# A transformer block's MLP: the second product by Strassen's seven as well, and its weight blocks prepared once in DRAM

## The chip, the core and the metric

One core of a Trainium2 chip runs one fused kernel. The metric is the device time of one execution in microseconds (us). TensorE (PE) does the matmuls, its weight loads stand as PEld; VectorE is DVE, ScalarE is ACT, GpSimd is POOL, SyncE is SP. SP, ACT and POOL also issue the DMAs, each from its own instruction queue.

## What is computed

The reference is one layer of a diffusion block over 2048 latent tokens of 1024 channels, with 256 context tokens. Cut to the part that changes:

```python
x   = x + g1 * mixed                                  # mixed: Fourier branch + neighbourhood attention, gated, projected
hx2 = modulate(rms_norm(x, norm2_g), sh2, sc2)        # 2048 x 1024
a   = relu(hx2 @ w_mlp1)                              # w_mlp1: 1024 x 4096
x   = x + g2 * ((a * a) @ w_mlp2)                     # w_mlp2: 4096 x 1024
```

Everything ahead of it (modulation vectors, the input projection, the Fourier transform, the attention, the gated merge) is computed by the same kernel.

## The kernel before, in words

**The stages.** The kernel runs through an input stage (projections of all tokens, pair by pair in `run_pair`), the Fourier transforms, the attention, a merge stage and the MLP. `merge` takes tiles t = 0 to 7 of 256 tokens: `attn_out(t)` gates and merges the branches, `out_proj` multiplies by w_out and adds the residual, `norm_T(t)` normalises, transposes and writes the operands of the MLP to DRAM (`hcd`).

**Numbers in halves.** Every fp32 operand is split into an f16 high and an f16 low part, so one logical matmul is three (`mm3`, L78: high by high, high by low, low by high). `halve` (L1446 on ACT, L1447 on DVE) makes the two parts of a weight block, with a power-of-two scale from `msc`.

**Seven products.** The first MLP product uses Strassen's scheme in Winograd's form: both operands are cut into 2 by 2 blocks, seven block products are formed from sums and differences of blocks, and sums of the seven give the four output blocks. `norm_T` makes the seven token operands (`put`, `total`). `load_w1` makes the seven weight operands of one pair of 128 hidden columns: one 1 MB DMA, four sums (L1425) and seven splits. `mlp1` runs the seven products (`product`, twelve matmuls of 128x512 each), adds them (`plus`, L1457), and makes relu, square and the f16 parts (`squared`, L1471 to L1475).

**The second product** is plain. `load_w2` splits 128 rows of w_mlp2, `mlp2` multiplies. Tokens go in two halves of 1024; in each half the hidden columns go in groups of four blocks of 128: two units of `mlp1`, then sixteen PSUM tiles (`order2`) of twelve matmuls, each added to an accumulator in SBUF (`acc`). The weights are loaded, summed and split again for the second half of the tokens.

**What sets the order.** A scheduler orders each engine's instructions when the program is built; `tc.issue_after` pins some behind others, the MLP's matmuls among them. Each engine then executes its list in order. The side work of the input stage (`side_work`: modulation vectors, maxima of the MLP weights) is a generator; every `tick()` in `run_pair` advances it, at `pace` 3 (three steps per two ticks) for the second pair and 2 (one per tick) after it. `mmp` and `p2p` are PSUM pools of four tiles each, so a product can start when the fourth product ahead of it has been read out.

Of the kernel before, what the change touches and what calls it, by code (L numbers as in the profile page):

```python
# [32 lines left out]
WTOP = 32768.0  # L33
# [3 lines left out]
ATOP = 181.0  # L37

PRODUCTS = (0, 5, 6, 4, 3, 2, 1)
# [20 lines left out]
def dit_block(ctx: ExitStack, tc: tile.TileContext, a, out, taps=None, upto=9):  # L60
# [54 lines left out]
    hcd = scratch("hcd", [2, 7, 128, 4, 1024], F16)  # L115
# [166 lines left out]
    def side_work():  # L282
# [67 lines left out]
        for i, top in enumerate((BTOP, BTOP, WTOP, ATOP)):  # L350
            dve.tensor_scalar(out=m[:, i:i + 1], in0=m[:, i:i + 1], scalar1=1.0e-12, scalar2=2.0 / top, op0=ALU.max, op1=ALU.mult)
# [7 lines left out]
        dve.tensor_scalar(out=g2r, in0=g2r, scalar1=msc[:, 4:5], scalar2=None, op0=ALU.mult)  # L359

# [969 lines left out]
    def norm_T(t, q_=sp):  # L1330
# [19 lines left out]
        def put(c, src):  # L1350
# [3 lines left out]
            q_.dma_start(hcd[t // 4, c, :, t % 4], o.rearrange("p o k t -> p (o k t)"))  # L1354
# [36 lines left out]
    load_x1()  # L1391
    for t in range(NT - 2):
        out_proj(t, 0)
        out_proj(t, 1)
        for _ in attn_out(t + 2, mmp, pg):
            pass
        norm_T(t)
    pm.release()
# [8 lines left out]
    w1, w2 = a["w_mlp1"][0], a["w_mlp2"][0]  # L1407

    def load_hc(half, part):
        r = {}  # L1410
        for c in (PRODUCTS[:4], PRODUCTS[4:])[part]:
            r[c] = (pr if part else pl).tile([128, 4, 2, 4, 128], F16, tag=f"hc{c}", name=f"hc{half}_{c}")
            sp.dma_start(r[c].rearrange("p s o k t -> p s (o k t)"), hcd[half, c])
        return r

    def load_w1(half, f, p_):

        nm = f"{half}_{f}"
        wt = pl.tile([128, KT, 256], F32, tag="w1r", name=f"w1r{nm}", bufs=2)
        sp.dma_start(wt, w1[:, f * 128:(f + 2) * 128].rearrange("(k p) n -> p k n", p=128))  # L1420
        a11, a12, a21, a22 = (wt[:, 4 * k:4 * k + 4, i * 128:(i + 1) * 128] for i in range(2) for k in range(2))

        def total(c, x, y, op):
            r = pl.tile([128, 4, 128], F32, tag="ws", name=f"ws{nm}_{c}", bufs=3)
            dve.tensor_tensor(out=r, in0=x, in1=y, op=op)  # L1425
            return r

        r = {}

        def put(c, src):  # L1430
            r[c] = p_.tile([128, 2, 4, 128], F16, tag=f"wc{c}", name=f"wc{nm}_{c}")
            halve(r[c][:, 0], r[c][:, 1], src, msc[:, 0:1])

        put(0, a11)
        s1 = total(4, a21, a22, ALU.add)
        s2 = total(5, s1, a11, ALU.subtract)
        put(5, s2)
        put(6, total(6, a11, a21, ALU.subtract))
        put(4, s1)
        put(3, a22)  # L1440
        put(2, total(2, a12, s2, ALU.subtract))
        put(1, a12)
        return r

    def halve(hi, lo, src, scale):
        act.activation(hi, src, AF.Copy, scale=scale)  # L1446
        dve.scalar_tensor_tensor(out=lo, in0=src, scalar=scale, in1=hi, op0=ALU.mult, op1=ALU.subtract)  # L1447

    def product(c, wc, hc, nm):
        ps = mmp.tile([128, 512], F32, tag="mm", name=f"pm{nm}_{c}")  # L1450
        w, h = wc[c], hc[c]
        with tc.issue_after(last_mm[0].ins):
            mm3(ps, [(w[:, 0, k], w[:, 1, k], h[:, :, 0, k], h[:, :, 1, k]) for k in range(4)])
        return ps

    def plus(o, x, y):
        dve.tensor_tensor(out=o, in0=x, in1=y, op=ALU.add)  # L1457
        return o

    def mlp1(half, f, wc, hc):  # L1460
# [3 lines left out]
        def room(tag, p_):  # L1464
            return p_.tile([128, 512], F32, tag=tag, name=f"{tag}_{nm}")

        r = {}

        def squared(o, x, y, i, j):
            plus(o, x, y)  # L1470
            act.activation(o, o, AF.Relu, scale=msc[:, 3:4])  # L1471
            act.activation(o, o, AF.Square)
# [17 lines left out]

    hid = {}
    t = NT - 2
    wc0 = load_w1(0, 0, pl)
    hc = load_hc(0, 0)
    out_proj(t, 0)
    out_proj(t, 1)
# [135 lines left out]
```

## Time and profile before

| | us |
|---|---|
| median of 3 runs | 2765.7 (2761.68 to 2765.79) |
| the profiled execution | 2767.06 |
| its span | 2765.3 |

The profiled execution by stage, from the windows view:

| stage | from - to | PE busy | DVE busy |
|---|---|---|---|
| input, up to the values' pair | 0 - 453 | 432.21 | 321.48 |
| values' pair | 453 - 557 | 98.86 | 26.28 |
| first keys' pair | 557 - 650 | 89.91 | 58.31 |
| second keys' pair | 650 - 742 | 92.00 | 47.92 |
| last gates' pair | 742 - 831 | 89.00 | 30.97 |
| Fourier transform | 831 - 887 | 52.57 | 20.77 |
| attention | 887 - 1206 | 298.42 | 270.08 |
| merge | 1206 - 1488.5 | 272.53 | 197.13 |
| MLP | 1488.5 - 2765.3 | 1250.95 | 743.26 |

A matmul's own duration is longer than the distance to the next one, since they are pipelined: 2688 matmuls of 381 ns each make 588.5 us of busy time. So what a matmul costs is read from a long unbroken row of them in the chain of waits (its length by its count), not from its mean duration.

### The profile page before, as it was taken

What the parts mean: (1) busy time and instruction counts of PE and PEld (TensorE: products, weight loads), DVE (VectorE), ACT (ScalarE), POOL (GpSimd) and SP (SyncE); (2) the same over time, 40 slices, a digit from 0 to 9 for tenths busy, and PEclk for the clock granted to TensorE, in tenths of its full rate; (3) what the DMA queues carried; (4) which work ended last, traced back from release to release, by engine and by line L of the source; (5) the groups of instructions that cost most, each with busy time, mean ns of one, the idle gap of its engine ahead of it and who ended that gap; (6) DMA issues with size and microseconds to landing.
All of it is one profiled execution on the core that took longest, in us unless ns stands there. A gap on an engine that the chain in (4) does not pass through costs nothing.

```text
span 2765.3 us, 41669 instructions
## 1 busy us (share of the span) xinstructions
PE 2643.2 (96%) x16209; PEld 1601.2 (58%) x16209; DVE 1716.2 (62%) x3380; ACT 1185.0 (43%) x2073; POOL 346.4 (13%) x486
## 2 busy tenths in 40 slices
PE   7899978999998899989998899999999999999999
PEld 5445656867647688878885344444444444444444
DVE  7746974255524888886666556665558456665536
ACT  5623326333313778853444544443333444443322
POOL 1201211011216454510000000000000000000000
PEclk9999999999998999999999999999999999999999
DMA  8577788352336455566666311211117221111102
GB/s 259 150 219 203 216 250 285 130 158 77 97 124 169 111 163 155 173 204 216 214 218 237 116 61 61 61 47 61 49 59 255 65 62 61 62 48 60 46 1 99
DMA packets 280862, 366.66 MB, mean 133 GB/s; under 512 B 38769, under 2 KB 217161, under 8 KB 276313
## 3 DMA queue, kind: packets, MB, share of 16 engines
q1 hardware_dynamic: 263913, 337.27, 38.9%
q0 software_dynamic: 11264, 16.76, 2.4%
q10 hardware_dynamic: 5488, 9.98, 1.0%
q8 instruction: 127, 2.08, 0.3%
q14 instruction: 70, 0.57, 0.1%
HBM read 277.83 MB, written 87.12 MB: 132 GB/s over the span
## 4 chain that ended last, share of the span: by engine, by line
PE 76%; DMA 9%; DVE 6%; issue 2%; ACT 1%; POOL 1%; SPq 0%; ACTq 0%; DVEq 0%; POOLq 0%
PE p L78 24%; PE pm L78 20%; PE ps_g L78 8%; PE po L78 6%; DMA w12m<-in_w_mlp 3%; PE pua L78 3%; PE ps_k L78 3%; PE tp L1181 2%; PE ps_v L78 2%; PE pmf L1119 2%; PE pv L1195 2%; PE sc L1159 1%; DMA wm<-in_wmask 1%; PE sc L1162 1%; DMA Q<-qH 1%
## 5 line engine op out<-in xcount | busy, mean ns | idle before, releaser
L78 PE MATMUL pm<-hc,wc 128*128 128x512 f16 x2688 | 588.5, 381 | 19.8 <-ACT p L1479 9.5
L78 PEld LDWEIGHTS <-wc 128*128 128x128 f16 x2688 | 264.0, 98 | 341.3 <-issue 27.7
L78 PE MATMUL p<-w2H,aH 128*128 128x512 f16 x1024 | 388.1, 379 | 0.0
L78 PE MATMUL p<-w2L,aH 128*128 128x512 f16 x1024 | 388.1, 379 | 0.0
L78 PE MATMUL p<-w2H,aL 128*128 128x512 f16 x1024 | 388.1, 379 | 0.0
L1457 DVE TENSOR_TENSOR acc<-p,acc 128x512 f32<-128x512 f32 x224 | 154.9, 691 | 318.4 <-PE p L78 318.1
L78 PE MATMUL ps_g<-hx,w_g 128*128 128x512 f16 x1536 | 343.2, 381 | 0.8 <-ACT ot_f L419 0.8
L78 PEld LDWEIGHTS <-aH 128*128 128x128 f16 x2048 | 200.4, 98 | 241.6
L1446 ACT ACTIVATE w2H<-w2s,msc 128x1024 f16<-128x1024 f32 x64 | 70.6, 1140 | 442.6 <-PE p L78 435.8
L78 PEld LDWEIGHTS <-hx 128*128 128x128 f16 x2304 | 227.4, 99 | 41.1 <-issue 5.3
L78 PEld LDWEIGHTS <-w_g 128*128 128x128 f16 x1536 | 151.1, 99 | 172.2 <-issue 4.3
L78 PEld LDWEIGHTS <-aL 128*128 128x128 f16 x1024 | 100.2, 98 | 120.8
L947 POOL DMA_DIRECT2D bt<-tT x264 | 132.3, 508 | 75.8 <-DVE ri L1188 59.1
L1447 DVE SCALAR_TENSOR_TENSOR w2L<-w2s,msc,w2H 128x1024 f16<-128x1024 f32 x64 | 80.7, 1282 | 91.9 <-ACT w2H L1446 91.9
L1446 ACT ACTIVATE wc<-ws,msc 128x512 f16<-128x512 f32 x128 | 91.2, 716 | 105.8 <-PE pm L78 103.1
L1168 DVE CUSTOM_DVE_ANT_0 s<-sc,bt,qsc 128x736 f32<-128x736 f32 (+5 forms) x128 | 111.2, 869 | 37.3 <-PE sc L1162 33.8
L419 ACT ACTIVATE ot_g<-ps_g,usc_g 128x512 f32<-128x512 f32 x64 | 43.7, 684 | 188.7 <-PE ps_g L78 177.9
L1189 DVE SCALAR_TENSOR_TENSOR pL<-tp,pH 128x640 f16<-128x640 f32 (+1 forms) x128 | 112.2, 877 | 6.7 <-ACT pH L1184 6.5
L1172 ACT ACTIVATE s<-s,m 128x736 f32<-128x736 f32 (+5 forms) x128 | 104.4, 816 | 15.2 <-DVE m L1168 14.7
L78 PE MATMUL po<-wouH,mH 128*128 128x512 f32 x256 | 101.0, 398 | 7.1 <-DVE ga L1238 7.1
L1181 PE MATMUL tp<-ident,s 128*128 128x128 f32 x704 | 104.7, 283 | 2.6 <-ACT s L1172 2.4
L78 PE MATMUL po<-wouH,mL 128*128 128x512 f32 x256 | 100.2, 393 | 0.0
(494 smaller groups left out, 4685.6 us busy)
## 6 DMA issues: line engine op xcount, KB each, us to landing
w12m<-in_w_mlp SPq DMA_DIRECT2D x32, 1024.0 KB
w1r<-in_w_mlp SPq DMA_DIRECT2D x32, 1024.0 KB
w2s<-in_w_mlp SPq DMA_DIRECT2D x64, 512.0 KB
gT<-ot_g SPq DMA_DIRECT2D x64, 256.0 KB
hc<-hcd SPq DMA_DIRECT2D x14, 1024.0 KB
hcd<-ho SPq DMA_DIRECT2D x42, 256.0 KB
x<-in_x SPq DMA_DIRECT2D x20, 512.0 KB
ws_g<-in_w_branch_gate SPq DMA_DIRECT2D x16, 512.0 KB
```

Of the source, the lines that this page charges most:

```text
L78: last_mm[0] = pe.matmul(ps, l, r, start=(start and i == 0), stop=(stop and i == n - 1))
L419: act.activation(o, ps, func, scale=scale)
L947: load_(t[i * 16:(i + 1) * 16, :, off + j0 * w:off + (j0 + 8) * w], raw(tT[ct], (2 * hp * 15 + dr) * w, [[120 * w, 16], [15 * w, 2], [1, 8 ...
L1119: pe.matmul(ps, l, r, start=(i == 0), stop=(i == len(prods) - 1))
L1168: tail["dve"] = dve.tensor_tensor_reduce(out=s[:, :n], in0=sc, in1=bias, op0=ALU.add, op1=ALU.min, scale=qsc[:, 4:5], scalar=3.0e38, accum ...
L1172: tail["act"] = act.activation(s[:, :n], s[:, :n], AF.Exp, bias=m1[:, 0:1], scale=-1.0, accum_out=m1[:, 1:2])
L1181: tail["pe"] = pe.transpose(tp[:, i * 128:(i + 1) * 128], s[:, o:o + 128], ident)
L1189: tail["dve"] = dve.scalar_tensor_tensor(out=pL[:, :c], in0=tp[:, :c], scalar=PTOP, in1=pH[:, :c], op0=ALU.mult, op1=ALU.subtract)
L1195: tail["pe"] = pe.matmul(pv, p_[:nk, i * 128:(i + 1) * 128], vv[:nk, h2 * 128 + o:h2 * 128 + o + 64], start=(j == 0 and i == 0), stop=(j = ...
L1446: act.activation(hi, src, AF.Copy, scale=scale)
L1447: dve.scalar_tensor_tensor(out=lo, in0=src, scalar=scale, in1=hi, op0=ALU.mult, op1=ALU.subtract)
L1457: dve.tensor_tensor(out=o, in0=x, in1=y, op=ALU.add)
```

## The change

**Both products by seven.** `mlp2` now also works by Strassen's seven. Four units of `mlp1` come first; each makes, beside the four blocks of squared activations, the three sums that the scheme needs, and splits all seven (`parts`). Then for each of the seven products c and each of four token sub-tiles s, twelve matmuls (four pairs of hidden blocks by three) are summed in one PSUM tile, and that tile is added to one or two of four accumulators (`X`). That is eight blocks of 128 hidden columns, "eight tiles summed in PSUM" where it was four. Of the first c the fourth pair's matmuls come after those of the other three, for all s.

**Weight blocks made once.** `prepare` makes the seven f16 blocks (high and low, 256 KB each) of a pair of hidden blocks: one job is one 1 MB load, 4 sums and 7 splits, in 7 steps, and 7 stores to DRAM (`w1d`, `w2d`). There are 32 jobs, sixteen for each weight matrix. Ten run as further side work of the input stage (loads and stores on SP's queue), six in the merge stage from t = 1 on (loads on SP, stores on POOL), sixteen beside the first half of the MLP (loads on ACT, stores on POOL). In the last two the raw tile is single: the next load is issued when the job before has read all of it.

**A ring of 15.** The MLP reads blocks by single 256 KB loads on SP's queue into a ring of 15, each issued where the one that had the room is last used, for both halves of the tokens: 448 loads.

**Smaller edits.** The scales' tops are lowered, so that sums fit in f16; `hcd` is one tile for each half; the last three products of `mlp1` come in the order 1, 3, 2; at the end x1 is loaded and the output stored by 128x512 quarters.

```diff
-PRODUCTS = (0, 5, 6, 4, 3, 2, 1)
+PRODUCTS = (0, 5, 6, 4, 1, 3, 2)
+PRODUCTS2 = (0, 1, 4, 5, 2, 6, 3)
...
+    prepared, N_EARLY, N_MERGE = set(), 10, 6
+    jobs = [(kind, f + o) for f in range(0, FF // 128, 8) for kind in (1, 2) for o in range(0, 8, 2)]
...
+    def prepare(todo, raw_room, sum_room, out_room, load_, dma, ahead):
...
+            def put(c, src):
+                flush()
+                o = out_room(f"wo{nm}_{c}")
...
+                halve(d[:, 0], d[:, 1], src, msc[:, 0:1] if kind == 1 else msc[:, 2:3])
+                out_.append(((w1d, w2d)[kind - 1][f // 2][c], o.rearrange("p o n -> p (o n)")))
...
+            for j, (c, o, ops) in enumerate(order):
+                if ops:
+                    total(o, *ops)
+                put(c, o)
...
+                if j == 1 and ahead:
+                    fetch(n + 1)
+                yield
+            if n + 1 == len(todo):
+                flush()
+            elif not ahead:
+                fetch(n + 1)
+                yield
...
+        yield from prepare(jobs[:N_EARLY], ..., sp.dma_start, sp.dma_start, True)
...
+    prep = prepare(jobs[:N_MERGE], ..., sp.dma_start, pool.dma_start, False)
     for t in range(NT - 2):
         out_proj(t, 0)
+        if t:
+            next(prep, None)
         out_proj(t, 1)
         for _ in attn_out(t + 2, mmp, pg):
-            pass
+            if t:
+                next(prep, None)
...
+    for half in range(2):
+        for f in range(0, NF, GF):
+            pairs = tuple(range(f, f + GF, 2))
+            slots += [(1, half, f1, c) for f1 in pairs for c in PRODUCTS]
+            slots += [(2, half, f, 0, s, pairs[:-1]) for s in range(4)] + [(2, half, f, 0, s, pairs[-1:]) for s in range(4)]
+            slots += [(2, half, f, c, s, pairs) for c in PRODUCTS2[1:] for s in range(4)]
...
+        wbs[b] = t = pl.tile([128, 2, 512], F16, tag="wb", name=f"wb{kind}_{half}_{f}_{c}", bufs=RING)
+        with tc.issue_after(ring_load[0].ins) if ring_load[0] else nullcontext():
+            ring_load[0] = sp.dma_start(t.rearrange("p o n -> p (o n)"), (w1d, w2d)[kind - 1][f // 2][c])
...
+        a21 = squared(u4, product(2), u4)
+        t = plus(room("at"), a21, a22)
+        parts(4, t)
+        plus(t, t, a11, ALU.subtract)
+        parts(5, t)
+        plus(a12, a12, t, ALU.subtract)
+        parts(2, a12)
+        plus(a21, a11, a21, ALU.subtract)
+        parts(6, a21)
...
+        for f1 in pairs:
+            h, w = hid[half, f1][c], wbs[2, half, f1, c]
+            with tc.issue_after(last_mm[0].ins):
+                mm3(ps, [(h[:, 0, cs], h[:, 1, cs], w[:, 0], w[:, 1])], f1 == f, f1 == f + GF - 2)
...
+    todo, steps = 8 * len(jobs), 0
+    horizon = next(i for i, s in enumerate(slots) if s[:4] == (2, 0, NF - GF, 0)) - RING
...
+        with behind_last(anchors, "dve"), behind_last(anchors, "act"):
+            while steps * horizon < i * todo and next(prep, "end") is None:
+                steps += 1
```

In DVE's list at the start of the MLP, behind the last `norm_T`, the kernel before has this (`c` and `u` are sums of products, `pm` is a PSUM tile of `mlp1`, `wc`, `ws` and `w1r` belong to `load_w1`, `ho` to `norm_T`):

```order
L1353 TENSOR_TENSOR ho_1_18321<-tm_18261,ho_1_18321 128x512
L1457 TENSOR_TENSOR c_0_0_18395<-pm_0_4_18240,u_0_0_18255 128x512
L1447 SCALAR_TENSOR_TENSOR wc_2_0_18341<-w1r_2_18339,msc,wc_2_0_18341 128x512
L1447 SCALAR_TENSOR_TENSOR wc_2_5_18348<-ws_2_5_18346,msc,wc_2_5_18348 128x512
L1425 TENSOR_TENSOR ws_2_2_18362<-w1r_2_18339,ws_2_5_18346 128x512
L1447 SCALAR_TENSOR_TENSOR wc_4_5_18472<-ws_4_5_18470,msc,wc_4_5_18472 128x512
L1457 TENSOR_TENSOR c_0_0_18394<-pm_0_3_18403,u_0_0_18255 128x512
...
L1447 SCALAR_TENSOR_TENSOR w2L_18371<-w2s_18372,msc,w2H_18370 128x1024
```

The changed kernel has this at the same place (`raw`, `ws`, `wo` belong to `prepare`, `p` is the first product's copy):

```order
L1431 TENSOR_TENSOR ho_1_18865<-tm_18805,ho_1_18865 128x512
L1551 TENSOR_TENSOR a_0_3_18926<-a_0_0_18804,a_0_3_18926 128x512
L414 TENSOR_TENSOR ws_16_18889<-raw_16_18887 128x512
L376 SCALAR_TENSOR_TENSOR wo_16_0_18890<-raw_16_18887,msc,wo_16_0_18890 128x512
L376 SCALAR_TENSOR_TENSOR wo_16_4_18897<-ws_16_18889,msc,wo_16_4_18897 128x512
L1551 TENSOR_TENSOR p_0_0_18746<-pm_0_1_18907,p_0_0_18746 128x512
L414 TENSOR_TENSOR ws_16_18889<-ws_16_18889,raw_16_18887 128x512
L376 SCALAR_TENSOR_TENSOR wo_16_5_18933<-ws_16_18889,msc,wo_16_5_18933 128x512
L376 SCALAR_TENSOR_TENSOR wo_16_1_18958<-raw_16_18887,msc,wo_16_1_18958 128x512
L1551 TENSOR_TENSOR u_0_0_18776<-pm_0_3_18936,u_0_0_18776 128x512
```

The splits of the second unit's weights and of w_mlp2 are gone from between the reads of `pm`; what stands there now is the first job of `prepare`, which waits for a raw load.

In DVE's list in the merge stage, behind the first projection tile, the kernel before has (`ga` is the gated branch, `pua` its PSUM tile, `ft` and `gf` are loaded):

```order
L1321 TENSOR_TENSOR x_128_15672<-po_1_1_15765,x_128_15672 128x512
L1238 TENSOR_TENSOR ga_0_15808<-pua_0_15815,ga_0_15808 128x256
L86 TENSOR_TENSOR mL_15807<-ga_0_15808,mH_15806 128x256
L1239 TENSOR_TENSOR ga_0_15808<-ga_0_15808,ft_0_15810 128x256
L1238 TENSOR_TENSOR ga_2_15849<-pua_2_15856,ga_2_15849 128x256
L1231 TENSOR_TENSOR ft_4_15892<-ft_4_15892,gf_4_15891 128x512
```

The changed kernel has there:

```order
L1316 TENSOR_TENSOR ga_0_16191<-pua_1_16215,ga_0_16191 128x256
L414 TENSOR_TENSOR wrooms<-raw_12_16482 128x512
L1316 TENSOR_TENSOR ga_2_16232<-pua_2_16239,ga_2_16232 128x256
L414 TENSOR_TENSOR raw_12_16482<-raw_12_16482 128x4x128
L1317 TENSOR_TENSOR ga_2_16232<-ga_2_16232,ft_2_16234 128x256
L376 SCALAR_TENSOR_TENSOR wrooms<-raw_12_16482,msc,wrooms 128x512
L1316 TENSOR_TENSOR ga_2_16232<-pua_3_16256,ga_2_16232 128x256
L376 SCALAR_TENSOR_TENSOR wrooms<-wrooms,msc 128x512
```

Eleven rows of a job (`wrooms` holds its sums and blocks) now stand between the reads of the PSUM tiles, 66 rows for the six jobs.

More of the change, by code (lines that the diff above doesn't have):

```diff
@@ L1412, in load_hc @@
             r[c] = (pr if part else pl).tile([128, 4, 2, 4, 128], F16, tag=f"hc{c}", name=f"hc{half}_{c}")
[L1413 removed]
+            sp.dma_start(r[c].rearrange("p s o k t -> p s (o k t)"), hcd[half][c])
         return r
[L1416 to L1443 removed]
@@ L1445, in halve @@
[L1445 to L1458, printed above, removed]
@@ L1499, in dit_block @@
     out_proj(t + 1, 1)
-    first = mlp1(0, 0, wc0, hc)
-    next(first)
+    units[0, 0] = mlp1(0, 0)
+    for _ in range(4):
+        next(units[0, 0])
     norm_T(t + 1, act)
```

300 lines of the change are left out of this document (211 added, 89 removed).

## The prediction, as it was put on record before the run

> **What bounds the kernel now.** I read the page first, for the share of each engine and its course over the span.
>
> ```profile
> span 2765.3 us, 41669 instructions
> PE 2643.2 (96%) x16209; PEld 1601.2 (58%) x16209; DVE 1716.2 (62%) x3380; ACT 1185.0 (43%) x2073; POOL 346.4 (13%) x486
> ...
> PE   7899978999998899989998899999999999999999
> ```
>
> PE is the bound, and from slice 23 on it never falls below nine tenths. The windows view (each engine's busy time, its instructions in brackets, then granted clock, DMA share, GB/s) says how closely, by stage:
>
> ```profile
> core 0: us, PE busy (x) PEld busy (x) DVE busy (x) ACT busy (x) POOL busy (x), PEclk, DMA share, GB/s
> ...
> 1240.00:1415.00 175.00, 175.00 (x1035) 155.39 (x1034) 120.03 (x243) 71.82 (x125) 9.25 (x11) 1.00 0.63 212
> 1488.50:1553.00 64.50, 43.93 (x186) 19.31 (x186) 52.85 (x78) 40.87 (x63) 0.55 (x1) 0.84 0.70 232
> 1553.00:2115.00 562.00, 562.00 (x2606) 254.77 (x2605) 320.55 (x457) 220.59 (x334) 0.00 (x0) 1.00 0.22 72
> 2115.00:2720.00 605.00, 605.00 (x2805) 274.29 (x2804) 337.05 (x481) 230.64 (x348) 0.00 (x0) 1.00 0.18 56
> ```
>
> In the MLP, PE is busy 562.00 of 562.00 and 605.00 of 605.00 us at a granted clock of 1.00, while DVE has 43% free; only the first 64.5 us of the stage are broken. So there a matmul taken away is time taken away, as long as nothing else becomes late. The chain of waits gives the price of one:
>
> ```profile
> 1537.59 3.44 DMA w2s<-in_w_mlp
> 1541.05 1.15 ACT w2H L1446
> 1542.73 10.35 PE pm L78 x36
> 1553.08 41.44 PE p L78 x192
> 1594.52 36.26 PE pm L78 x168
> ...
> 2682.32 36.26 PE pm L78 x168
> 2718.58 41.45 PE p L78 x192
> 2760.06 0.70 DVE acc L1457
> 2760.78 0.70 DVE acc L1570
> ```
>
> From 1553.08 to 2760.06 the chain holds PE alone: 41.44 / 192 = 36.26 / 168 = 0.2158 us for a matmul.
>
> **A. The matmuls.** PE's list is 384 matmuls shorter: a half took 8 groups of 168 + 192, and takes 4 groups of 336 + 336; 2 x (2880 - 2688) = 384. At 0.2158 us that is **-82.9 us**. Nothing else could take part of that away but waits, which follow. That a product costs as much in the new row as in the old is safe: shapes and types are the same.
>
> **B. The start of the MLP.** Of the first 64.5 us, 168 matmuls of the MLP need 36.3; 28.3 are lost. The timeline (start, length, engine and queue, line, operation, idle time before it) shows where:
>
> ```profile
> 1495.74 16.46 SPq L1413 DMA_DIRECT2D hc<-hcd  x3
> ...
> 1501.66 2.75 PE L78 MATMUL pm<-hc,wc 128*128 128x512 f16 x12
> ...
> 1511.12 5.28 PE L78 MATMUL pm<-hc,wc 128*128 128x512 f16 x12 [6.71 <-DMA hc<-hcd]
> 1511.88 1.20 ACT L1352 ACTIVATE ho<-tm 128x512 f16<-128x512 f32 x2 [3.76 <-DMA hcd<-ho]
> ```
>
> Three operand loads and the norm's last stores hold PE until 1511; weight splits (chain rows, up to 1541) hold it after. The splits are gone now, and `hcd` by halves frees the loads of `hc` from the last norm_T's stores. Two new waits stand there. On SP, the loads of `hc` 1, 3 and 2 are queued behind the ring loads that wait for the end of the fourth product; that is at about 1499, and an operand issued at 1495.74 let PE go on at 1501.66, 5.9 us later, so PE stands for about that long. On DVE, the first job of `prepare` waits for its raw load, issued on ACT's queue behind norm_T at about 1514, some 6 us more; behind it in DVE's list stands the read of `pm`, and after three more PSUM tiles PE waits for that: I follow some 7 us. With 4 us for the transposes of the last norm_T between, my walk through the lists gives 16.8 lost in place of 28.3: **-11.5 us**. Bounds: 0 (the new waits cost all that the splits did) and -20 (one of the two is covered).
>
> **C. The merge.** The six jobs put 66 DVE rows (24 sums, 42 splits), 42 ACT rows and 17.3 MB into t = 1 to 5. The groups of the tile `w1r` give the durations (min/median/max in ns); the waits of DVE in 1240 to 1415 show what it waits for already:
>
> ```profile
> L1446 ACT ACTIVATE wc<-w1r,msc x96: 705/714/724, 1449.3 to 2640.9; 128x512 f16<-128x512 f32 x96
> L1447 DVE SCALAR_TENSOR_TENSOR wc<-w1r,msc,wc x96: 745/751/754, 1451.2 to 2641.7; 128x512 f16<-128x512 f32 x96
> L1425 DVE TENSOR_TENSOR ws<-w1r x64: 680/689/697, 1448.5 to 2622.3; 128x512 f32<-128x512 f32 x64
> ```
>
> ```profile
> DVE ft L1231 <- DMA ft<-mF: 10.6, 12, 2.4
> ```
>
> 24 x 0.689 + 42 x 0.751 = 48.1 us; with the 120.03 there, DVE has 168 of 175 us. The DMAs go from 212 GB/s at a share of 0.63 to 212 + 17.3 MB / 175 us = 311 GB/s, by proportion a share of 0.93. PE is at 175.00 of 175.00 there, so every wait of it is lost time. Three more things are in order: the first sum waits for its raw load with the read of `pua` queued behind it, the single raw tile lets the next load go only when the job has read it, and the stores stand on POOL ahead of the norms' `rs_b`. Then, at the passage to the MLP, 15 ring loads and 4 MB of `hc` stand ahead of the norms' stores on the engines. From below: 0, since all fits on paper. From above: six jobs, each with a wait like the longest for `ft` (2.4 us) and one more of the same, are 29, of which PSUM's other tiles cover a part: 20. I take **+7**, nearer to nothing, as one wait of 2.4 us for half of the jobs is the nearest row.
>
> **D. The input stage.** Ten jobs are stepped there, in the keys' pairs above all:
>
> ```profile
> 557.00:650.00 93.00, 89.91 (x641) 63.59 (x639) 58.31 (x168) 33.52 (x65) 18.44 (x18) 0.98 0.51 153
> 650.00:742.00 92.00, 92.00 (x662) 64.98 (x661) 47.92 (x151) 24.90 (x51) 19.43 (x20) 1.00 0.23 70
> ```
>
> About 38 DVE rows fall into the first keys' pair: 38 x 0.729 (mean of the durations above) = 27.7, and DVE has 86 of 93 us. 17 fall into the second: 60 of 92. The rest lie where DVE has more room. The first pair loses 3.1 us already; **+4**, bounds 0 and 12 (DVE's 86 us in the worst order with the waits for ScalarE).
>
> **E. The first half's preparation.** Sixteen jobs run beside the first half's products. The windows of one phase each of before:
>
> ```profile
> 1594.50:1630.80 36.30, 36.30 (x170) 16.43 (x168) 30.58 (x44) 24.84 (x39) 0.00 (x0) 1.00 0.27 87
> 1630.80:1672.20 41.40, 41.40 (x193) 18.78 (x192) 13.91 (x21) 5.02 (x8) 0.00 (x0) 1.00 0.09 26
> ```
>
> Two units of `mlp1` had 44 DVE rows in 36.3 us, 30.58 of them busy, and PE lost nothing. A unit of seven products now has 18 rows of its own and six of a job: 24 in 84 x 0.2158 = 18.1 us, and 18 x 0.69 + 6 x 0.729 = 16.8, 93%. In the product phases each PSUM tile takes 12 x 0.2158 = 2.59 us and brings DVE at most two sums, 1.4 us, so there is room. A raw load comes late for a job by up to 6 us (B); four PSUM tiles give PE 3 x 2.59 = 7.8 us. **+4** for sixteen jobs, bounds 0 and 30 (2 us each).
>
> **F. Ring and tail.** 448 loads of 256 KB, one per 2.59 us of PE, are 101 GB/s; fifteen blocks cover 39 us. With the raw loads and stores of the half (16 x (1.05 + 1.84) MB in 520 us, 89 GB/s) that is 190, under the 232 and 212 that windows above sustain: 0. At the end each last tile brings two sums and the output's add: **+1**, -1 to 3.
>
> On a row against this change: small DMAs of before show how long one takes from issue to landing (last column, us),
>
> ```profile
> mF<-mo POOLq DMA_DIRECT2D x16, 512.0 KB, 4.0
> ...
> bt<-tT POOLq DMA_DIRECT2D x176, 24.0 KB, 3.2
> ```
>
> so a block of 256 KB lies between 3.2 and 4.0 us, longer than the 2.59 that PE needs one for. It is the basis of the third rival. The Trainium skill ("DMA: Bandwidth & Descriptors", section "Bandwidth") says to gather DMAs into 1 MiB or more for three quarters of the peak, which speaks against cutting the weights into blocks; by the fit in its section on the SWDGE path, 2.0 us plus bytes at 436 GB/s, one is 2.6 us, an estimate, and the ring would run level with PE or just behind. The trace's 3.2 to 4.0 us are longer than that fit.
>
> **Sum.** 2767.06 - 82.9 - 11.5 + 7 + 4 + 4 + 1 = 2688.7. The profiled execution stands 1.4 over the median of the runs shown, so 2687 beside it.
>
> **The rivals.**
> 1. *The early jobs saturate DVE and the DMAs* (merge and first keys' pair): C at 20 and D at 12 give 21 more than the forecast, 2708; with B at nothing, 2720. For it: 168 of 175 and 86 of 93 us, both with in-order waits for loads. Against: the same engine ran 44 rows in 36.3 us without a loss, 84% busy.
> 2. *DVE becomes the bound of `mlp1` in the first half.* 16.8 us of rows plus eleven hand-overs from ACT, each as the waits in the MLP show it,
>
> ```profile
> DVE wc L1447 <- ACT wc L1446: 28.1, 57, 1.2
> ```
>
> 28.1 / 57 = 0.49 us, make 22.3 for a unit against PE's 18.1: 4.2 x 16 = 67 us, so about 2750 in place of E's 4. It decides if most splits of DVE wait for their ACT half. Against: before had more hand-overs per us.
> 3. *Slower: the ring's loads run one behind the other.* All stand on SP's one queue, each waiting for a room. If a load starts only when the one ahead has landed, 448 x 3.2 = 1434 us against 5376 x 0.2158 = 1160 of PE: +273, so about 2959. It is slower than before from (1160 + 80) / 448 = 2.77 us per load on. Against: the windows of before hold 212 and 232 GB/s, mostly with loads of 0.25 to 1 MB on SP, which at 256 KB is 1.1 to 1.2 us for one; so loads overlap.
>
> That the change doesn't do what it says is excluded: the list is 384 matmuls shorter, and the same scheme ran for the first product.
>
> **How the numbers follow.** Forecast 0.62 (2664 to 2705: B and C to E at their gentler bounds); rival 1 0.18 (2705 to 2722); rival 2 0.13 (2728 to 2770, around 2750); rival 3 0.04; better than all bounds 0.03. The range goes from 2662 (-82.9 - 20 - 1 and nothing lost elsewhere) to 2728, and leaves out rival 2's most, rival 3 and a little below: 0.2. A measurement of this kernel tells 0.2%, 5.5 us, from no change. All cases but rival 3 are faster by more: faster 0.95, same 0.01 (rival 2 at its very worst), slower 0.04.
>
> **What the profile after would show.** Right: in the chain, rows of 336 matmuls of 72.5 us for either product with PE alone between, 145.0 per group; about 17 us of PE's gaps behind 1488, ended by `hc` and by DVE's reads; in the merge and the first keys' pair PE's gaps of some us in all; DVE at 85 to 93% in the first half's `mlp1`; PE never waiting for a ring block. Wrong: PE waiting for `wb` (rival 3), PE waiting for DVE once per product in the first half (rival 2), or gaps in the merge over 20 us (rival 1). A row of 336 matmuls longer than 72.5 us would unseat A itself.

## The result, and the profile after

The changed kernel takes **2735.0 us** (median of 4 runs, 2730.59 to 2738.39), the kernel before 2765.7; the ratio is 0.989, interval 0.9873 to 0.9908. It is faster by 31 us, where 79 were forecast, and its time lies above the range. The profiled execution is 28.7 us shorter than that of before by their spans:

```profile
span 2736.6 us, 42696 instructions
## 1 busy us (share of the span) xinstructions
PE 2572.6 (94%) x15825; PEld 1567.7 (57%) x15825; DVE 1813.5 (66%) x3628; ACT 1180.4 (43%) x2105; POOL 456.7 (17%) x688
## 2 busy tenths in 40 slices
PE   6899988898999799988999799999999999999998
```

PE has 384 instructions fewer, as forecast, but its busy share fell from 96 to 94%: it waits more. The row of slices shows where, counted from 0: slice 22, in which the merge passes into the MLP, was an eight and is now a seven, and ahead of it nine slices are under nine tenths where eight were.

**Where the 28.7 us are.** I take the start times of four matmuls from the trace (the first of the Fourier transform, of the output projection, and of the MLP, and the MLP's n-th), and compare what lies between. In the MLP, n matmuls at the forecast's 0.2158 us are taken off, so that what is left is lost time.

| term of the forecast | before | after | measured | forecast |
|---|---|---|---|---|
| D: to the first matmul of the Fourier transform | 830.7 | 851.4 | +20.7 | +4 |
| from there to the first output projection | 399.8 | 401.1 | +1.3 | 0 |
| C: from there to the MLP's first matmul | 258.0 | 278.1 | +20.2 | +7 |
| B: lost in the first phase of `mlp1` | 28.2 | 24.1 | -4.1 | -11.5 |
| A: matmuls of the MLP | 5760 | 5376 | -82.9 | -82.9 |
| E: lost in the rest of the first half | 0 | 13.8 | +13.8 | +4 |
| lost in the second half, up to the last group | 0 | 0 | 0 | 0 |
| F: last group, beyond its matmuls | 5.4 | 7.7 | +2.3 | +1 |
| sum | | | -28.7 | -78.4 |

The windows view of the changed kernel, cut at those matmuls (first `mlp1` phase, first `mlp2` phase, second and third group, then all to the last group), shows the MLP's part:

```profile
core 0: us, PE busy (x) PEld busy (x) DVE busy (x) ACT busy (x) POOL busy (x), PEclk, DMA share, GB/s
1530.70:1627.20 96.50, 78.45 (x353) 35.37 (x353) 64.39 (x103) 50.47 (x82) 8.16 (x15) 0.93 0.68 217
1627.20:1706.40 79.20, 74.35 (x337) 33.21 (x336) 45.78 (x70) 30.62 (x51) 11.36 (x21) 0.98 0.55 184
1706.40:1853.00 146.60, 145.14 (x673) 65.73 (x672) 107.54 (x167) 63.05 (x99) 18.93 (x35) 1.00 0.62 199
1853.00:2003.70 150.70, 146.61 (x675) 66.08 (x673) 107.47 (x167) 63.05 (x99) 18.92 (x35) 0.99 0.59 195
2003.80:2656.50 652.70, 652.70 (x3026) 295.86 (x3024) 357.77 (x550) 212.36 (x337) 23.77 (x44) 1.00 0.42 133
```

From 2003.8 on PE is busy for 652.70 of 652.70 us; the last column but one shows the DMAs at 0.42 there, with the ring running. DVE in the second and third group is at 107.5 of 147 and 151 us, far from full, and yet PE loses time in those groups. So it is not an average that binds there. The chain of waits has the rows that were forecast from the fourth group on:

```profile
2003.85 72.52 PE pm L78 x336
2076.37 72.52 PE p L78 x336
...
2584.01 72.52 PE pm L78 x336
2656.53 49.23 PE p L78 x228
2705.78 1.35 DVE X L1551 x3
```

72.52 / 336 = 0.2158 us: term A holds to the hundredth. At the end the chain leaves PE at 2705.78 for DVE's sums, so the tail is DVE's.

The start of the MLP in the timeline (start, length, engine and queue, operation, in brackets the idle time before it and what ended it):

```profile
1547.53 8.12 SPq L1511 DMA_DIRECT2D hc<-hcd  x3
...
1554.06 4.29 PE L78 MATMUL pm<-hc,wb 128*128 128x512 f16 x12 [9.92 <-DMA hc<-hcd]
...
1557.09 0.52 ACTq L387 DMA_DIRECT2D raw<-in_w_mlp  x1
...
1570.17 0.69 DVE L414 TENSOR_TENSOR ws<-raw 128x512 f32<-128x512 f32 x1 [11.16 <-DMA raw<-in_w_mlp]
1570.18 0.72 ACT L375 ACTIVATE wo<-raw,msc 128x512 f16<-128x512 f32 x1 [11.89 <-DMA raw<-in_w_mlp]
...
1573.06 3.26 PE L78 MATMUL pm<-hc,wb 128*128 128x512 f16 x10 [3.99 <-DVE p L1551]
```

Both waits that the prediction named are there, in the order it named. The raw load was to take some 6 us: issued at 1557.09, it let DVE and ACT go on at 1570.17, 13.1 us later, beside three operand loads and ring loads; but PE stood only 3.99 us behind it, where some 7 were forecast. The operand load was to be issued as the fourth product ends; that was about 1541, and it went at 1547.53. SP's own waits say what held it and the two behind it (total, times, longest):

```profile
SPq L1511 <- DMA hcd<-ho: 13.1, 3, 6.8
```

The three loads (L1511) went at 1547.53, 1554.69 and 1555.33, each as a store of the last `norm_T` (`hcd<-ho`) landed.

Three gaps are left in the first half behind its first phase. The longest stands early in the first `mlp2` phase, and it is ACT's, not DVE's:

```profile
1620.04 0.38 ACTq L387 DMA_DIRECT2D raw<-in_w_mlp  x1
...
1626.04 0.72 ACT L375 ACTIVATE wo<-raw,msc 128x512 f16<-128x512 f32 x1 [4.18 <-DMA raw<-in_w_mlp]
...
1641.52 2.51 ACT L1555 ACTIVATE X<-p 128x512 f32<-128x512 f32 x5
...
1642.62 17.55 PE L78 MATMUL p<-wb,a 128*128 128x512 f16 x73 [4.85 <-ACT X L1555]
```

A raw load is issued on ACT's queue, the next row of ACT but one needs it and stands 4.18 us; everything behind it is late by that, and 16 us on PE waits 4.85 us for ACT to read out the first PSUM tile of `mlp2`. The other two gaps (1.46 and 4.09 us) stand at the same place in the second and third group, and there DVE reads the tile:

```profile
PE p L78 <- DVE X L1551: 5.5, 2, 4.1
PE p L78 <- ACT X L1555: 4.9, 1, 4.9
```

```profile
1767.40 5.93 DMA raw<-in_w_mlp
...
1917.40 5.81 DMA raw<-in_w_mlp
```

Ahead of these two as well ACT stood for a raw load, 4.18 and 4.06 us. PE comes to this place after the first product's 48 matmuls, and the order of the change leaves little cover there: the last twelve of the 48 finish the four PSUM tiles three matmuls apart, so 9 matmuls, 1.9 us, lie between the end of the first tile and the matmul that needs its room.

In the merge, the waits of PE, then those of DVE and of ACT on the raw loads (total, times, longest):

```profile
PE po L78 <- DVE ga L1316: 15.2, 5, 7.0
PE tpb L1418 <- DVE tm L1423: 3.6, 1, 3.6
```

```profile
DVE wrooms L414 <- DMA raw<-in_w_mlp: 11.6, 5, 3.7
```

```profile
ACT wrooms L375 <- DMA raw<-in_w_mlp: 21.8, 5, 6.7
```

7.0 of the first row stood there before too (7.1). The rest, some 12 us of PE's gaps, is new: PE waits for a gated branch that DVE and ACT finish late, and both stand for a raw load at nearly every job. Behind three of these gaps (4.78, 3.63 and 2.56 us) the granted clock is half for 3.4 us; in the kernel before it is 1.00 from 1233.6 us to the end of the stage. Some 5 of the 20.2 us are matmuls that come more slowly there.

### The profile page after: what moved, and what is told of

Read it like the earlier page. It is cut to its first block, busy times and chain, and to the rows that moved or that the text cites. A ratio compares the mean times of both kernels' runs of the same rounds, so it can differ in the third digit from the quotient of the medians.

```text
span 2736.6 us, 42696 instructions
## 1 busy us (share of the span) xinstructions
PE 2572.6 (94%) x15825; PEld 1567.7 (57%) x15825; DVE 1813.5 (66%) x3628; ACT 1180.4 (43%) x2105; POOL 456.7 (17%) x688
## 4 chain that ended last, share of the span: by engine, by line
PE 62%; DMA 14%; DVE 13%; issue 4%; ACT 4%; SPq 2%; POOL 1%; ACTq 0%; DVEq 0%; POOLq 0%
PE p L78 19%; PE pm L78 16%; PE ps_g L78 8%; PE po L78 4%; DMA w12m<-in_w_mlp 4%; DMA raw<-in_w_mlp 4%; PE tp L1259 2%; PE ps_k L78 2%; PE pmf L1197 2%; PE ps_f L78 2%; PE pv L1273 2%; SPq L178 1%; PE sc L1237 1%; PE pua L78 1%; DVE wo L376 1%
## 5 line engine op out<-in xcount | busy, mean ns | idle before, releaser
L78 PE MATMUL pm<-hc,wb 128*128 128x512 f16 x2688 | 585.5, 381 | 17.1 <-DMA hc<-hcd 12.5
L78 PE MATMUL p<-wb,a 128*128 128x512 f16 x2688 | 584.9, 380 | 10.4 <-DVE X L1551 5.5
L78 PEld LDWEIGHTS <-wb 128*128 128x128 f16 x2688 | 263.7, 98 | 337.3 <-issue 23.1
L78 PEld LDWEIGHTS <-a 128*128 128x128 f16 x2688 | 263.7, 98 | 330.3 <-issue 15.3
L1551 DVE TENSOR_TENSOR X<-X,p 128x512 f32<-128x512 f32 x280 | 184.2, 685 | 219.7 <-PE p L78 194.1
L1551 DVE TENSOR_TENSOR u<-pm,u 128x512 f32<-128x512 f32 x128 | 87.9, 690 | 94.0 <-PE pm L78 91.6
L1555 ACT ACTIVATE p<-pm 128x512 f32<-128x512 f32 x32 | 19.0, 593 | 253.5 <-PE pm L78 253.5
L375 ACT ACTIVATE wo<-raw,msc 128x512 f16<-128x512 f32 x104 | 71.6, 712 | 114.1 <-DMA raw<-in_w_mlp 67.8
L375 ACT ACTIVATE wo<-ws,msc 128x512 f16<-128x512 f32 x78 | 56.2, 720 | 140.6 <-DVE ws L414 91.3
L1250 ACT ACTIVATE s<-s,m 128x736 f32<-128x736 f32 (+5 forms) x128 | 104.4, 816 | 15.9 <-DVE m L1246 15.5
L78 PE MATMUL po<-wouL,mH 128*128 128x512 f32 x256 | 102.2, 400 | 0.0
```

What stands on the lines that cost most here:

```text
L78: last_mm[0] = pe.matmul(ps, l, r, start=(start and i == 0), stop=(stop and i == n - 1))
L1250: tail["act"] = act.activation(s[:, :n], s[:, :n], AF.Exp, bias=m1[:, 0:1], scale=-1.0, accum_out=m1[:, 1:2])
L1551: last["dve"] = dve.tensor_tensor(out=o, in0=x, in1=y, op=op)
```

## The experiments

Three theories were held against each other for what the jobs cost. **L**: rows of DVE and ACT stand in order behind a raw load that has not landed. **R**: the rows themselves fill DVE and ACT. **D**: the bytes slow the stage's own loads and stores. Each run was one execution with a profile, unless said otherwise; the changed kernel's total was 2735.0 and that of before 2758 to 2765 beside them. "Input extra" and "merge extra" are the first and third line of the table above, against the kernel before. They have a spread of their own: over the kernels that leave a stage's jobs as they are in the changed kernel, the input extra lay between 12.4 and 21.2 us (ten kernels) and the merge extra between 18.7 and 20.2 (four).

**One load only.**

```diff
-                raws[n] = t = raw_room(f"raw{kind}_{f}")
+                if keep and n:
+                    raws[n] = kept[0]
+                    return
+                raws[n] = t = raw_room(f"raw{kind}_{f}")
+                kept.append(t)
```

> Leaves out: in the input stage and in the merge only the first job loads its raw weights; the other jobs work on the same raw tile, with all their sums, splits and stores. Theory L (late loads: ScalarE and VectorE stand in order behind a raw load that has not landed, and TensorE behind them): the input stage's extra 20.7 us shrink to 8 or less and the merge's extra 21 us to 6 or less; about 2705 us in all. Theory R (the rows themselves fill VectorE): both stay within 4 us of what they were, about 2733. Theory D (the traffic of loads and stores slows the stage's own loads): the loads are half of the jobs' bytes, so about half goes, 2715.

2715.8 us; input extra 7.5, merge extra 10.3. In the input stage 5 to 14 us are gone, measured against its spread, which is L's figure; in the merge half is gone, which is D's figure, as is the total. So neither theory holds for both stages.

**No rows.**

```diff
+                if bare:
+                    if not one:
+                        one.append(out_room(f"wo{nm}_{c}"))
+                        act.activation(one[0].rearrange("p o n -> p (o n)"), t0[:, :1024], AF.Copy)
+                    out_.append(((w1d, w2d)[kind - 1][f // 2][c], one[0].rearrange("p o n -> p (o n)")))
+                    return
```

> Leaves out: the jobs of the input stage and of the merge do all loads and all stores, but no sums and no splits; one copy on ScalarE per job stands for them. Theory L: VectorE no longer stands behind a load, only one row of ScalarE per job does, so most goes: input +6, merge +4, about 2703 in all. Theory R: the same, 2700. Theory D: both extras stay, within 5 us, about 2732. With the first run beside it: L if both are near 2705, R if only this one is, D if only this one is not.

2726.3 us; input extra 10.5, merge extra 20.0. In the input stage the extra is 2 us under its spread, so the rows may matter there; that is not more than a hint. For the merge the result speaks for D alone. Runs below show that neither the loads nor the stores cost as much in other company, but none repeats this one.

**The first half without jobs.**

```diff
-        while (kind, f) not in prepared:
+        f0, f = f, f % 16
+        while (kind, f) not in prepared:
...
-    todo, steps = 8 * len(jobs), 0
+    todo, steps, prep = 0, 1, iter(())
```

> Leaves out: the sixteen jobs beside the first half of the MLP; the blocks of the first sixteen hidden columns' blocks are read again in their place. If the jobs make the gaps of the first half, and the late first raw load the last gap at the MLP's start: 13.9 us of the first half and about 5 of the start go, 2716, and every row of 336 matmuls in the first half is 72.5 us. If the scheme's own rows on VectorE and ScalarE make them: no change, 2735.

2704.2 us. All of the first half's 13.8 us go, and the first phase loses 14.1 in place of 24.1. The chain of waits of this run from the start on:

```profile
1549.87 57.14 PE pm L78 x264
1607.01 72.52 PE p L78 x336
```

From 1549.87 PE never waits again. So the scheme's own rows on DVE and ACT fit, and each gap of the first half, with 10 us of the start, belongs to the jobs. Of these 10, 4.4 are operand waits: PE waits 8.1 us for `hc` here and 12.5 in the changed kernel.

**No jobs in the merge.**

```diff
-    prepared, N_EARLY, N_MERGE = set(), 10, 6
+    prepared, N_EARLY, N_MERGE = set(), 10, 0
```

> The six jobs of the merge stage go to the first half of the MLP, 22 jobs there. Theory L: the merge is as before (its extra 21 us go), the half pays 0.9 us for each of six more jobs (13.9 over 16): about 2719. Theory R: the 22 jobs' rows overfill VectorE in the half; the merge gains 21, the half loses 30 or more: 2744.

2720.8 us. Merge extra 0.2, so all 20 belong to the six jobs; the first half loses 22.5 behind its first phase in place of 13.8, and the first phase 29.7 in place of 24.1. A job costs 3.3 us in the merge and (8.7 + 5.6) / 6 = 2.4 beside the MLP, more than L's 0.9 and half of R's 5 or more; that the total still met L's figure is owed to the input stage, which had 8 us less extra in this run (12.4) with the same jobs. In this run alone PE's waits also name a ring block, twice, 2.8 and 2.5 us; the cause was not followed.

**Two raw tiles in the first half.**

```diff
-    RING, GF = 15, 8
+    RING, GF = 13, 8
...
-    prep = prepare(jobs, lambda n_: pr.tile([128, 2048], F32, tag="raw", name=n_), lambda n_: pr.tile([128, 512], F32, tag="wt", name=n_),
-                   lambda n_: small(n_).bitcast(F16).rearrange("p (o n) -> p o n", o=2), act.dma_start, pool.dma_start, False)
+    prep = prepare(jobs, lambda n_: pr.tile([128, 2048], F32, tag="raw", name=n_, bufs=2), lambda n_: pr.tile([128, 512], F32, tag="wt", name=n_),
+                   lambda n_: small(n_).bitcast(F16).rearrange("p (o n) -> p o n", o=2), act.dma_start, pool.dma_start, True)
```

> Beside the first half of the MLP two raw tiles in place of one, the next load issued while a job is worked on; the ring has 13 blocks to make room. Theory L for the half (its 13.9 us of gaps are waits for a raw load that is issued only when the job before has read its tile): the gaps go but for the first job's, -9 to -14, about 2723. Rival (the sums and splits crowd VectorE and ScalarE whenever they come): the gaps stay, 2735. A ring of 13 still covers 34 us: no wait of TensorE for a block.

2725.5 us. The gaps behind the first phase fall from 13.8 to 5.9 us, and 5.3 of these stand in the first group. With the same rows in the same place, the earlier loads take 8 us away, just under L's 9 to 14: L for the half. PE did not wait for the ring of 13.

**No stores in the merge, and none in the input stage.**

```diff
             while out_:
-                dma(*out_.pop(0))
+                o_ = out_.pop(0)
+                if store:
+                    dma(*o_)
```

> Leaves out: the 42 stores of the merge stage's six jobs; loads, sums and splits stay, and the MLP reads other blocks in their place. The merge's extra was 20.1 us with all, 10.3 with one load, 20.0 without rows, 0.2 without jobs. Theory D (traffic, by bytes): 6.3 of 17.3 MB are left, so about 7 us of the 20 stay, 2722 in all. Theory L (the late raw loads): 16 or more stay, 2731 or more.

> Leaves out: the 70 stores of the input stage's ten jobs; loads, sums and splits stay, and the MLP reads other blocks in their place. The stage's extra was 20.7 us with all (17.6 and 12.4 in two other kernels with the same jobs), 7.5 with one load, 10.5 without rows. Theory D: 10.5 of 28.9 MB are left, 6 to 8 us stay, about 2724. Theory L: 12 or more stay, 2729 or more.

2734.4 and 2725.7 us. In the merge 21.7 are left where 20.2 were: the stores cost nothing that shows. In the input stage 15.9 are left; in ten kernels that have the ten input jobs untouched, that extra lay between 12.4 and 21.2, so the stores are not shown to cost anything there. D had forecast 7 for both.

**All late jobs in the half, two raw tiles, a lead.** The fourth and fifth edits together, and three steps between the first raw load and the first row that reads it.

> No jobs in the merge; 22 in the first half of the MLP, with two raw tiles, a ring of 13, and three steps between the first raw load and the first row that reads it. If late raw loads make the half's gaps: the merge as in the kernel before (-20 from the changed kernel), the half's gaps down to 3 us or less (-11), the start 4 us shorter: about 2700. If the rows do: the half loses 20 or more with 22 jobs, 2722 or more.

2706.1 us: merge extra 0, gaps behind the first phase 1.7 us with 22 jobs. So the rows of 22 jobs fit beside the first half when their loads are early. The start did not improve (27.3): the steps of the lead had no other row of the MLP between them, and the rows still stood for the load (9.93 and 10.65 us in the timeline).

**A lead in the merge.**

```diff
-                fetch(n + 1)
-                yield
+                fetch(n + 1)
+                for _ in range(3 if load_ == sp.dma_start else 1):
+                    yield
```

> Five jobs in the merge in place of six (the sixth goes to the MLP's first half), and after each raw load's issue three steps in place of one before the first row that reads it, so that the load has some 10 us. Theory L (in the merge, rows stand behind a raw load issued just ahead of them): the merge's extra falls from 20 to 7 or less, about 2722. Theory B (the 1 MB load itself is a burst that holds up the stage's own small loads and stores, whenever it is read): five sixths stay, 16 or more, about 2731.

2720.7 us; merge extra 13.4 with five jobs (five sixths of 20.2 are 16.8). Neither figure was met, and the waits say why the run tells little: ACT still waited for raw loads four times, 16.7 us, and DVE four times, 9.3. Three steps of the program's order were not enough time, so L was not tested here.

**Jobs spread.** On the ninth run's kernel:

```diff
-    prepared, N_EARLY, N_MERGE = set(), 10, 0
+    prepared, N_EARLY, N_MERGE = set(), 8, 0
...
                 yield
+                if dma == sp.dma_start:
+                    yield
...
-            while steps * horizon < i * todo and next(prep, "end") is None:
+            while steps * (horizon - 12) < (i - 12) * todo and next(prep, "end") is None:
```

> The kernel of the ninth run, with eight jobs in the input stage in place of ten, one step every second tick in place of every tick, so they reach into the pairs behind the keys', where VectorE and the DMAs have room; 24 jobs in the first half of the MLP, the first not before the twelfth product. If density makes the input stage's extra: it falls from 20.5 to 10 or less; the start of the MLP falls from 27.3 to 20, since no row stands behind the first raw load while the operands load. About 2687. If the bytes make it wherever they go: input 16, 2700. If 24 jobs overfill the half: its gaps rise from 2 to 15 or more.

2673.8 us: input extra 4.1, merge 0.1, first phase 14.0, behind it 2.1. All of density's figures are met, and it is better than forecast at the start, where the jobs now come after the operand loads. Fewer jobs and half the density came together here, so this run does not tell one from the other.

**The raw loads in quarters.** On the tenth run's kernel, each 1 MB load as four of 256 KB.

> The kernel of the tenth run (five jobs in the merge, a lead of three steps), with each raw load cut into four loads of 256 KB, one or two per step: the same bytes and rows, no burst of 1 MB. Theory B (a 1 MB load holds up the stage's own loads and stores): the merge's extra falls from 13.4 to 7 or less, about 2714. If it is the sum of bytes and rows in the stage, whatever their order: it stays at 11 to 15, 2720.

2722.2 us; merge extra 17.7, above both figures. The bursts of 1 MB are gone and the extra is not, so theory B's figure fails. The last quarters left one step ahead of the rows, as in the changed kernel, and five sixths of its extra are 16.8.

**The spread kernel, timed.**

> The kernel of the eleventh run again, timed in five rounds: 2674 within 4 us, 0.967 of the kernel before (0.965 to 0.969); the input stage's extra 4 us, the merge's 0, the start's loss 14.

2679.6 us (2676.91 to 2680.82, 5 runs) against 2761.7 of the kernel before on the same chip: ratio 0.9695, interval 0.9681 to 0.9708. A little above what I expected (2674 within 4); the input stage's extra was 2.9, the first phase lost 16.5. This version beats the kernel before, and its median is 55 us under that of the changed kernel, which was timed beside another execution of the kernel before.

**The merge: loads alone, rows alone.**

```diff
-                if ops:
-                    total(o, *ops)
-                put(c, o)
+                if ops and rows:
+                    total(o, *ops)
+                if rows:
+                    put(c, o)
```

The second run keeps the rows, leaves out the stores as above, and has the first run's `keep` for the loads.

> Leaves out: in the merge stage the six jobs' sums, splits and stores; only their six loads of 1 MB stay, and nothing waits for them. If the bytes of the loads slow the stage's own loads and stores: an extra of 10 or more, as in the run without rows (20.0, where one row of ScalarE per job still waited for each load). If it is only the rows that wait for the loads: 3 or less.

> Leaves out: in the merge stage all stores and all loads but the first; the sums and splits of the six jobs stay, all on one raw tile. If the rows alone crowd VectorE and ScalarE (they then have 48 us more in 240): an extra of 8 or more, as with rows and stores (10.3). If the stores made that: 3 or less.

2717.4 and 2724.2 us; merge extra 2.0 with the loads alone (D had 10 or more) and 8.3 with the rows alone. The same 260 us of the merge, with loads alone, with rows alone, with both and no stores (the run above), and in the changed kernel:

```profile
1240.00:1500.00 260.00, 250.06 (x1424) 219.62 (x1423) 174.61 (x339) 102.49 (x176) 16.16 (x17) 0.99 0.73 256
```

```profile
1240.00:1500.00 260.00, 248.63 (x1391) 216.77 (x1392) 207.89 (x400) 126.57 (x215) 15.14 (x16) 0.98 0.68 233
```

```profile
1240.00:1500.00 260.00, 237.81 (x1330) 207.84 (x1331) 206.12 (x395) 123.15 (x209) 14.72 (x15) 0.96 0.70 237
```

```profile
1240.00:1500.00 260.00, 240.50 (x1360) 210.29 (x1359) 211.33 (x397) 123.97 (x212) 44.30 (x59) 0.97 0.82 280
```

With 256 GB/s and no rows PE loses little; with DVE at 208 of 260 us and no loads some more; together, at 237 GB/s and DVE at 206, PE loses far more than the two. So neither these bytes alone nor the rows alone make the 20.

| merge extra, us | rows | no rows |
|---|---|---|
| loads, no stores | 21.7 | 2.0 |
| no loads but the first, no stores | 8.3 | - |
| loads and stores | 20.2 | 20.0 (one row of ACT per job) |
| no loads but the first, stores | 10.3 | - |

Of the 20: 8 are the rows (R), 2 the loads by themselves (D), the stores 0 to 2, and 10 to 11 come only when rows and loads are there together. By the waits of DVE and ACT that is rows standing behind loads (L); no run of the merge had the same rows with early loads, so L is argued here and not shown. Part of the 10 to 11 is the slower clock behind longer gaps: PE's gaps alone grow by 2.8 us with the loads, 4.4 with the rows and 15.4 with both. One cell stays open: the run without rows has stores and one row of ACT per job behind its load, and loses 20.0. Its chain holds a store of the norm that took 16.23 us. So loads and stores with hardly a row can cost as much by another way; why was not settled.

## Why the prediction was wrong, point by point

- **A, the matmuls: right.** 0.2158 us for each, in unbroken rows of 336. The third rival (ring loads one behind the other) is out: PE never waits for `wb` in the changed kernel; it is SP that waits, 196 and 202 times from 1640 us on, for PE to free a room:

```profile
SPq L1543 <- PE p L78: 457.4, 202, 14.7
SPq L1543 <- PE pm L78: 425.0, 196, 2.2
```

- **B, the start: right places, wrong sizes; -4.1 in place of -11.5.** The step that cost most is that "`hcd` by halves frees the loads of `hc` from the last norm_T's stores". It did not: each of the three loads waited for such a store, 13.1 us in all, and the first left 6 us after the end of the fourth product. The stores go to the other half, so it is not the data; the loads' tiles lie where the norm's were, which fits, but was not tried. The time of the load itself was about right: 6.5 us from issue to PE, where 5.9 were taken (in the kernel before PE did the norm's transposes until 1501.7, so 5.9 was a bound and no wait). PE so waited 12.5 us for `hc` in place of 5.9. The raw load failed the other way about: it took 13.1 us, not some 6, but PE stood 4.5 behind it (3.99 and 0.55) and not 7. And some 3.3 us are matmuls at the lower clock, which the walk did not have. Without the jobs (third run) the first phase loses 14.1 and not 24.1.
- **C, the merge: +20.2 in place of +7.** The step "one wait of 2.4 us for half of the jobs is the nearest row" was mis-sized: the wait for `ft` is for a load of 256 KB, issued some 4 us ahead of its reader. A raw load of 1 MB is issued when the job before has ended, just ahead of its reader, stands in the chain of this stage with 7.87, 8.88 and 8.52 us, and DVE waited 11.6 us for five of six, ACT 21.8. And the rows alone, which "all fits on paper" put at 0, cost 8.3. The first rival had the size (20), with saturation of DVE and DMAs as its cause; the runs show that half of it comes only with rows and loads together, and that neither DVE's rows alone nor the loads' bytes alone make it; that it is the loads' lateness is read from the waits.
- **D, the input stage: +20.7 (12 to 21 in other kernels) in place of +4.** I counted DVE's rows by pairs and left the loads, ACT and the values' pair at nothing. PE's waits there in the changed kernel:

```profile
PE ps_v L78 <- ACT vo_v L627: 8.7, 4, 3.0
PE pu_g L475 <- DVE usc_k L476: 7.6, 2, 4.3
PE ps_k0c L78 <- DVE qn_k L558: 5.3, 1, 5.3
```

  Of the first, 4.7 us stood there before too. The second of these ends a string of a job's splits, in which ACT stood for a block's store to free its room; the third ends a wait of ACT for the values that the stage itself loads, which the kernel before has too (3.1 us of PE's there):

```profile
541.60 0.72 ACT L375 ACTIVATE wo<-raw,msc 128x512 f16<-128x512 f32 x1 [1.64 <-DMA w1d<-wo]
...
544.62 0.56 PE L475 MATMUL pu_g<-usc_g,ones 128*128 128x1 f32 x2 [4.27 <-DVE usc_k L476]
```

```profile
615.63 1.33 ACT L837 ACTIVATE vi<-vi,vsc 128x512 f16<-128x512 f32 x2 [3.17 <-DMA vi<-vF]
...
618.32 1.04 PE L78 MATMUL ps_k0c<-w_k,hc 128*128 128x256 f16 x4 [5.30 <-DVE qn_k L558]
```

  So loads, rows and rooms that wait for a store each stand in the way here: 7.5 were left with one load, 10.5 without rows, 2.9 and 4.1 with eight jobs at half the density. How much each has was not settled.
- **E, the first half: +13.8 in place of +4.** The failing step is the cover: "four PSUM tiles give PE 3 x 2.59 = 7.8 us". All three gaps stand at the one place where it is 1.9 us, behind the first product of `mlp2`. And ACT was left out: it stood 4.06 to 4.18 us for a raw load ahead of each of these gaps, and its rows of the jobs stand ahead of the rows that hand over from `mlp1` to `mlp2`. Two raw tiles took 8 of the 14 away, no jobs all. The second rival (0.49 us at each handover from ACT) did not happen: outside three places of the first half behind its first phase PE lost nothing.
- **F: right,** 2.3 where 1 was said.

One term was in no step: behind a long wait (in the MLP, of 3.99 us and more) the granted clock is halved, and the matmuls there cost more. By the distances between the starts of the MLP's matmuls, eight gaps (the norm's transposes in them) make 31.7 us of the 38 that the first three groups lose, and 6.2 are matmuls that came too slowly.

## What to carry to other kernels

A background job in an in-order list can cost more by its lateness than by its length: in the merge, 48 us of rows on a DVE with room for them cost 8 us of PE when they waited for no load, and 20 with their loads, where by the waits each job's first row stood behind a load that was issued just ahead of it, and the stage's own rows behind that. Issue such a load a whole job ahead (beside the MLP a second raw tile took 8 of 14 us away, and 22 jobs then cost less than 16 did), place the jobs where the stage has room rather than where they first fit, and count every engine that holds a row of the job. When the sure part of a forecast is a shorter list on the bounding engine, the rest of the error sits in the waits: size them by a load of the same size, issued as late, in the same traffic.

## What the runs showed of the hardware

**A long wait of PE costs more than its length.** The windows around the gap of 9.92 us, and of the first 4 us and the next 53.5 us behind that of 4.85 us, in the changed kernel:

```profile
1547.30:1557.50 10.20, 3.44 (x9) 1.23 (x9) 4.75 (x8) 3.21 (x6) 0.00 (x0) 0.51 0.80 229
```

```profile
1642.50:1646.50 4.00, 3.88 (x11) 1.42 (x11) 1.66 (x3) 3.60 (x8) 1.16 (x3) 0.57 0.86 257
1646.50:1700.00 53.50, 53.50 (x250) 24.23 (x249) 28.04 (x42) 13.40 (x21) 7.58 (x14) 1.00 0.59 201
```

The granted clock (the column behind POOL) is about half, in the last two rows for the first 3.4 us, then 1.00 again; by their starts the matmuls in such a stretch come 0.43 us apart in place of 0.2158. It was so behind the four gaps of the MLP of 3.99 us and more, and not behind those of 1.65 us and less; in the merge it was so behind one of 2.56 us too. The Trainium skill, "TensorE: Matmul & The Clock Gate", section "Part 1: The HAM clock gate (the "warmup" mystery)", says that the clock is halved after an idle window of about 3.4 us and comes back after a busy one; the traces agree for the four gaps of the MLP, while the one of 2.56 us in the merge is shorter than that window.

**A load of 1 MB under traffic took 5.6 to 13.1 us.** In the chain of waits of the changed kernel the raw loads of the first half stand with 13.06, 5.64, 5.93, 7.69 and 5.81 us. Stores of a block of 256 KB from POOL landed after 2.7 and 3.1 us beside the MLP and after 3.7 and 4.2 us in the merge (medians):

```profile
w1d<-wo POOLq DMA_DIRECT2D x56, 256.0 KB, 2.7
w2d<-wo POOLq DMA_DIRECT2D x56, 256.0 KB, 3.1
w2d<-wrooms POOLq DMA_DIRECT2D x28, 256.0 KB, 3.7
...
w1d<-wrooms POOLq DMA_DIRECT2D x14, 256.0 KB, 4.2
```

The first is near the 2.6 us which the fit of the Trainium skill ("DMA: Bandwidth & Descriptors", section "Anatomy of one DMA — SWDGE (gpsimd) path") gave in the prediction as an estimate; in the merge it is exceeded. The ring's own loads go by SP and not by that path.

**Loads of 256 KB on one queue overlap.** In the `mlp2` phases of the second half SP issues the ring's blocks in fours, 0.65 us apart (2250.58 to 2252.52), and by the trace the last packet of the four ends at 2255.79. So four are in within 5.2 us of the first issue, and PE, which needs one per 2.59 us, does not wait for them. The Trainium skill's rule, in section "Bandwidth" of that page, is to gather DMAs into 1 MiB or more; blocks of a quarter of that cost this kernel no wait of PE.
